# Two-layer backbone on one core: stores whose data ScalarE wrote last move from SyncE's DMA queue to ScalarE's own

## The chip, the cores and the metric

One Trainium2 chip, one of its cores. A core has TensorE (PE), VectorE (DVE), ScalarE (ACT), GpSimd (POOL) and SyncE (SP). SP does nothing but issue DMA transfers. ACT and POOL can issue them too. The metric is the device time of one execution, in microseconds.

## The reference

Two layers over 512 latent and 256 context tokens of 1024 channels. Each layer projects the normed tokens once, runs differential attention and a bidirectional gated DeltaNet on the result, merges both, and then runs PEER: every token picks, for each of 8 heads, 16 of 16384 experts. An expert is one row of `u` and one row of `v`.

```python
y = sigmoid(gA) * (da @ w_ba) + sigmoid(gB) * (dn @ w_bb);  x = x + gate1 * (y @ w_o)
# PEER, per block of 128 tokens; ib: 128 expert numbers of a token, gb: their gates
u   = jnp.take(u_tab, ib, axis=0)
act = jax.nn.gelu(jnp.einsum('tnd,td->tn', u, hb), approximate=False)
v   = jnp.take(v_tab, ib, axis=0)
out = jnp.einsum('tn,tnd->td', gb * act, v)
```

## The kernel before, in words

Matmul operands are split into a high and a low part, and each product takes three matmuls (high by high, low by high, high by low). A tile of a table comes by DMA into `wraw`, `uraw` or `vraw`; ACT casts the high part (`whi`, `uhi`, `vh`, line 189, here "L189"), and POOL or DVE subtracts to get the low part (`wlo`, `ulo`, `vl`, L167). PE multiplies at L160 and transposes at L164. ACT moves most results from PSUM to SBUF (L185, L189, L475, L1349).

The stretches of the span, with the times of the profiled execution: the mixer of layer 0 (0 to 1550 us), its PEER with routing first (1620 to 2260) and the main loop behind it (to 3450), then the mixer of layer 1 (3460 to 4620, with the merge from about 4430 on), and its PEER (scores from 4620, routing 4860 to 5260, main loop to 6080).

What the kernel writes to DRAM on the way:

- In the mixer, `inproj` writes each projected strip (`ev`) to `raw` or to the merge gates `Ga`. DeltaNet's `prep` writes normed keys, values and queries (`kvn`, `kq`). `da_head` writes one head's attention output (its tile is called `g` in the trace) to `AT`. The merge reads `AT` back into `ya`, ACT casts it to `mWh`, and PE multiplies. `norm_turn` writes the rows of the tokens that are gathered to `hrow`.
- In the routing stretch, `spread` builds a dense map of gates for 128 tokens from one-hot tiles: DVE makes `oh`, PE multiplies, ACT scales the result into `stg`, and each finished `stg` (4 MB) goes to `G` in DRAM, 14 times in all. Beside it run two streams: `own_u` gathers the expert rows of the tokens that are not done densely (POOL issues the gather `gb`, DVE multiplies and sums), and `peer_h` computes the first 80 of 128 blocks of `gelu(u . h)` for the dense tokens and keeps each in DRAM (`He`) until the main loop. These are called the blocks done ahead.
- In the main loop, `own_v` gathers rows of `v`, four tokens at a time, PE sums them, ACT copies the sums (`gev`, L1349), and they go to `own`.

Every transfer but the gathers is issued by SP through `load`, loads and stores in one queue of instructions. An engine executes its instructions in order, so a store on SP that waits for its tile holds what stands behind it.

No order is written by hand. The program goes through a list scheduler, which arranges the instructions of each engine by its own estimate of their times. So a change of the engine of a transfer can rearrange all engines. Tiles are numbered buffers: a tile with `bufs=2` is free again when the readers of its last use are done, and a store is a reader.

Of the kernel before, what the change touches and what calls it, by code (L numbers as in the profile page):

```python
# [108 lines left out]
class Ker:  # L109
# [45 lines left out]

    def load(self, dst, src, eng=None):
        (eng or self.nc.sync).dma_start(dst, src)

    def mm(self, out, lhsT, rhs, start=True, stop=True, **k):
        self.PE.matmul(out, lhsT, rhs, start=start, stop=stop, skip_group_check=True, **k)  # L160
# [200 lines left out]
    def norm_turn(self, pool, y, A, shift, hi, lo, toff, hi_on="v", lo_on="v", rows=None):  # L361
        for c0 in (0, 4):
            pt = self.psum("tp")
            hf = self.t(pool, [128, 4, 128], "nhf", bufs=2)
            for c in range(4):
                self.tr(pt[:, c * 128:(c + 1) * 128], y[:, (c0 + c) * 128:(c0 + c + 1) * 128])
            for c in range(4):
                self.act(hf[:, c], pt[:, c * 128:(c + 1) * 128], AF.Identity, scale=A[:, c0 + c:c0 + c + 1],
                         bias=shift[:, c0 + c:c0 + c + 1])
            ts = slice(toff, toff + 128)  # L370
            self.split(hi[:, c0:c0 + 4, ts], lo[:, c0:c0 + 4, ts], hf, hi_on, lo_on)
            if rows is not None:
                if c0 == 0:
                    hb = self.t(pool, [128, D], "nsq", bufs=1)
                pt = self.psum("tp")
                for c in range(4):
                    self.tr(pt[:, c * 128:(c + 1) * 128], hf[:, c])
                self.S.copy(hb[:, c0 * 128:c0 * 128 + 512], pt)
        if rows is not None:
            self.load(rows, hb)  # L380

    def inproj(self, pool, l, tile_i, hT, T, dst, kind=None):


        ps = self.parts("ip", T)
        self.proj(ps, self.wload(self.I["w_in"][l, tile_i], NCH), hT, step=256)
        u = self.t(pool, [128, 768], "ev", bufs=2)[:, :T]
        if kind == "silu":
            th = self.t(pool, [128, 768], "ev", bufs=2)[:, :T]
        for p, o, n in ps:  # L390
            x = slice(o, o + n)
            if kind == "tanh":
                self.act(u[:, x], p, AF.Tanh, scale=0.5)
            elif kind == "silu":
                self.act(th[:, x], p, AF.Tanh, scale=0.5)
                self.act(u[:, x], p, AF.Copy, scale=0.5)
            else:
                self.act(u[:, x], p, AF.Copy, scale=kind or 1.0)
        if kind == "silu":
            self.stt(u, th, 1.0, u, ALU.add, ALU.mult)  # L400
        self.load(dst[:, :T], u)


    @stream("a")
    def da_head(self, pool, l, h, raw, full, AT, lamc, subc):
        li = 0.8 - 0.6 * math.exp(-0.3 * l)
        TQ_ = 768 if full else 512
# [86 lines left out]
            self.tr(pt[:, i * 128:(i + 1) * 128], o2[:, i * 128:(i + 1) * 128])  # L494
        of = self.t(pool, [128, 768], "g2", bufs=2)
        self.act(of[:, :TQ_], pt[:, :TQ_], AF.Copy, scale=subc)
        self.load(AT[:, h, :], of[:, :TQ_])

    def lam_col(self, keep, pool, l):
        li = 0.8 - 0.6 * math.exp(-0.3 * l)  # L500
# [95 lines left out]
    @stream("p")  # L596
    def dn_prep(self, pool, l, h, wi, raw, cw, full, QKd, Knd, Vnd):

        T = 512 if (wi == 0 and not full) else 768
        nt = T // 128  # L600
        th = self.dn_conv(pool, l, h, raw, wi, cw, T)
        off = [i * 128 + (4 if i >= 4 else 0) for i in range(nt)]
        pt = self.psum("sc")
        for i in range(nt):
            self.tr(pt[:, i * 128:(i + 1) * 128], th[:, off[i]:off[i] + 128])
        p3 = pt[:, :T].rearrange("p (a b) -> p a b", b=128)
        dst = self.t(pool, [128, 6, 128], "kvn", bufs=2)[:, :nt]
        if wi == 2:
            self.act(dst, p3, AF.Copy, scale=0.5)
            self.load(Vnd[h], dst)  # L610
            return
        s2 = self.t(pool, [128, 6, 128], "kvn", bufs=2)[:, :nt]
        ss = self.sm(nt)
        for i in range(nt):
            self.act(s2[:, i], p3[:, i], AF.Square, accum=ss[:, i:i + 1])
        self.ts(ss, ss, 0.25, EPS, ALU.mult, ALU.add)
        r = self.sm(nt)
        self.rsqrt(r, ss, nt)
        self.ts(r, r, 0.5 * (128 ** -0.5 if wi == 0 else 1.0), None, ALU.mult)
        for i in range(nt):  # L620
            self.act(dst[:, i], p3[:, i], AF.Copy, scale=r[:, i:i + 1])
        if wi == 1:
            self.load(Knd[h], dst)
        pb = self.psum("at")
        for i in range(nt):
            self.tr(pb[:, i * 128:(i + 1) * 128], dst[:, i, :])
        kT = self.t(pool, [128, 6, 128], "kq", bufs=1)[:, :nt]
        self.S.copy(kT, pb[:, :T].rearrange("p (a b) -> p a b", b=128))
        self.load(QKd[wi][h][:, :nt], kT)

    def dn_solve(self, pool, U):

# [243 lines left out]
    def mixer(self, l, full, xin, xm, h2, near, hT, S, N):  # L876
# [97 lines left out]
        for h in range(2):  # L974
            u = self.t(ep, [128, 768], "ev", bufs=2)
            for p, o, n in first[h][1]:
                self.S.copy(u[:, o:o + n], p)
            self.load(raw[TDK][h], u)
        with P("dv", N) as pool:
            vec = self.dn_vectors(mp, pool, l, hT)  # L980
        bp = dn.enter_context(P("dnb", S))
# [274 lines left out]
    def spread(self, pool, ixs, gate, i, Gd, tick):  # L1256

        V, pair = self.V, self.pair
        n128 = lambda tag: self.t(pool, [128, 128], tag, bufs=1)

        pt = self.psum("tp")
        for x in range(2):
            self.tr(pt[:, x * 128:(x + 1) * 128], ixs[x])
        self.tr(pt[:, 256:384], gate)
        dup = self.t(pool, [128, 4, 128, 2], "rdup", F16, bufs=2)
        self.S.copy(dup[:, 0:2], pair(pt[:, 0:256].rearrange("p (a b) -> p a b", b=128)))
        g14 = n128("rg14")
        self.act(g14, pt[:, 256:384], AF.Copy, scale=GSCALE)
        g16 = self.t(pool, [128, 128], "rg16", F16, bufs=1)
        self.S.copy(g16, g14)  # L1270
        V.tensor_copy(dup[:, 2], pair(g16))
        self.tt(g14, g14, g16, ALU.subtract)
        V.tensor_copy(dup[:, 3], pair(g14))
        every = lambda k, t: dup[:, k, t:t + 8].unsqueeze(2).broadcast_to([128, 8, 64, 2])
        io = self.iota.rearrange("p (a b) -> p a b", b=2).unsqueeze(1).broadcast_to([128, 8, 64, 2])
        for half in range(2):
            stg = self.t(pool, [128, 128, 64], "stg", bufs=2)
            for t8 in range(8):
                oh = self.t(pool, [128, 3, 8, 128], "oh", F16, bufs=3)
                t = half * 64 + t8 * 8  # L1280
                o4 = oh.rearrange("p k t (a b) -> p k t a b", b=2)
                self.tt(o4[:, 0], io, every(1, t), ALU.is_equal)
                self.tt(o4[:, 1], io, every(0, t), ALU.is_equal)
                self.tt(o4[:, 2], o4[:, 1], every(3, t), ALU.mult)
                self.tt(o4[:, 1], o4[:, 1], every(2, t), ALU.mult)
                n = 8 if t8 % 2 else 4
                for u0 in range(0, 8, n):
                    pg = self.psum("at" if t8 % 2 else "tp")
                    for u in range(n):
                        o = pg[:, u * 128:(u + 1) * 128]  # L1290
                        self.mm(o, oh[:, 0, u0 + u], oh[:, 1, u0 + u], stop=False)
                        self.mm(o, oh[:, 0, u0 + u], oh[:, 2, u0 + u], start=False)
                    v = t8 * 8 + u0
                    self.act(stg[:, :, v:v + n].rearrange("p i t -> p t i"),
                             pg.rearrange("p (t i) -> p t i", i=128), AF.Copy, scale=1.0 / GSCALE)
                tick(1 + t8 % 2)
            self.load(Gd[2 * i + half], stg)


    def fetch(self, src, ix):  # L1300
# [34 lines left out]
    def own_v(self, l, own, out):  # L1335

        for s in range(0, 128, 4):
            bs = []
            for q in range(4):
                bs.append(self.fetch(self.I[f"v{l}"], own["ixT"][:, s + q:s + q + 1]))  # L1340
                if q < 3:
                    yield
            ev = self.t(self.gp, [128, D], "gev", bufs=1)
            for o in (0, 512):
                ps = self.psum("tp")
                for q in range(4):
                    self.mm(ps[32 * q:32 * q + 32, :], own["w"][:, s + q:s + q + 1].broadcast_to([128, 32]),
                            bs[q][:, o:o + 512], tile_position=(0, 32 * q))
                self.S.copy(ev[:, o:o + 512], ps)  # L1349
            self.load(out[s:s + 4, :], ev[0:128:32, :])  # L1350
            yield

    def own_all(self, l, owns, rows, outs):
# [27 lines left out]
    def peer(self, l, hT, h2, hg, rows, groups, ahead, near, S, N):  # L1381
# [12 lines left out]
        with ExitStack() as es:  # L1394
# [4 lines left out]
            with P("rt", N) as pool:  # L1399
# [19 lines left out]
                for b in range(ahead):  # L1419
                    ge = self.peer_h(l, b, hT, TT)  # L1420
                    Hd[b] = self.t(self.dp, [128, TT], f"He{l}_{b}")
                    self.load(Hd[b], ge)
            main = ExitStack()
            gp = main.enter_context(P("pg", N))
            adp = main.enter_context(P("ada", N))
# [214 lines left out]
```

## Time and profile before

| | |
|---|---|
| device time, median of 3 runs | 6079.62 us (6079.35 to 6086.33) |
| the profiled execution: time, span | 6081.79 us, 6080.0 us |
| mean granted TensorE clock | 0.969 |
| PE busy | 5620.5 us, 92% of the span |
| DVE, ACT, POOL busy | 4169.0, 2407.6, 2008.7 us |
| DMA moved | 1253.53 MB, 206 GB/s on the mean |

The median and the profiled execution differ by 2.17 us. PE is idle for 6080.0 - 5620.5 = 459.5 us of the span. Issuing a DMA does not count as busy time.

### The profile page before, as it was taken

Reading aid. Unit: us, or ns where it says so; the run is one execution under the profiler, and the core shown is the slowest. Engines: PE = TensorE matmul, PEld = TensorE weight load, DVE = VectorE, ACT = ScalarE, POOL = GpSimd, SP = SyncE. Lnnn points to the kernel's source line nnn. Section 1 sums busy time; section 2 is a strip of 40 time slices with the busy share of each in tenths; the row PEclk is TensorE's granted clock in tenths of the full one; section 3 lists DMA queues with packets and bytes.
Section 4 is the critical chain, followed back from the end, with each engine's and each line's share of the span. In section 5 each row is a group of like instructions: output and inputs, shape, how many; then the busy total and the mean of one; then the engine's idle time right before and its main releaser. Section 6 shows DMA issues by size and latency. Waiting matters only on the chain. (4 is left out here: it accounts for less than half of the span.)

```text
span 6080.0 us, 98316 instructions
## 1 busy us (share of the span) xinstructions
PE 5620.5 (92%) x36087; PEld 4639.6 (76%) x36087; DVE 4169.0 (69%) x9095; ACT 2407.6 (40%) x4320; POOL 2008.7 (33%) x1833
## 2 busy tenths in 40 slices
PE   8999999998888999999999899999999977599998
PEld 6888888777767787666666588888877977587776
DVE  5889886335789876665644669888745599765445
ACT  4554444323224542222233445444533335333333
POOL 2333333231264313333433433334441153312221
PEclk9999999999999999999999999999999998799999
DMA  5442323542278888998988644322254378977886
GB/s 189 154 141 92 100 94 105 173 154 86 69 256 299 293 307 305 333 346 312 328 302 278 224 144 148 118 96 93 96 168 139 125 262 300 329 241 270 286 277 215
DMA packets 567859, 1253.53 MB, mean 206 GB/s; under 512 B 65936, under 2 KB 228432, under 8 KB 565584
## 3 DMA queue, kind: packets, MB, share of 16 engines
q1 hardware_dynamic: 456784, 844.54, 41.0%
q0 software_dynamic: 110592, 402.70, 18.8%
q8 instruction: 284, 4.65, 0.3%
q14 instruction: 199, 1.63, 0.1%
HBM read 1049.76 MB, written 197.23 MB: 205 GB/s over the span
## 5 line engine op out<-in xcount | busy, mean ns | idle before, releaser
L167 POOL TENSOR_TENSOR wlo<-wraw,whi 128x512 fp32r<-128x512 f32 x418 | 571.9, 1371 | 1390.3 <-ACT whi L189 1257.7
L160 PE MATMUL ip<-hhi,whi 128*128 128x256 f32 x3120 | 736.5, 293 | 28.7 <-ACT ev L185 22.4
L160 PE MATMUL ip<-hlo,whi 128*128 128x256 f32 x3120 | 736.3, 291 | 0.7 <-POOL hlo L167 0.7
L160 PE MATMUL ip<-hhi,wlo 128*128 128x256 f32 x3120 | 729.0, 291 | 4.5 <-POOL wlo L167 4.4
L160 PEld LDWEIGHTS ip<-hhi,whi 128*128 128x128 f32 x3120 | 521.2, 192 | 43.0 <-ACT ev L185 26.2
L167 DVE TENSOR_TENSOR acc<-acc,tp 128x512 f32<-128x512 f32 x366 | 247.8, 684 | 445.5 <-PE tp L160 444.6
L160 PE MATMUL ip<-h2hi,ulo 128*128 128x512 f32 (+1 forms) x1408 | 521.4, 371 | 32.9 <-DVE ulo L167 32.9
L160 PE MATMUL ip<-h2hi,uhi 128*128 128x512 f32 (+1 forms) x1408 | 522.3, 371 | 29.6 <-ACT uhi L189 28.9
L160 PEld LDWEIGHTS ip<-hhi,wlo 128*128 128x128 f32 x3120 | 521.2, 193 | 14.9 <-POOL wlo L167 5.5
L189 ACT CAST uhi<-uraw 128x1024 fp32r<-128x1024 f32 x256 | 269.3, 1052 | 663.9 <-PE ip L160 386.8
L160 PEld LDWEIGHTS ip<-hlo,whi 128*128 128x128 f32 x3120 | 524.1, 192 | 8.9 <-POOL hlo L167 1.0
L160 PE MATMUL ip<-h2lo,uhi 128*128 128x512 f32 (+1 forms) x1408 | 519.4, 369 | 0.0
L1302 POOL DMA_INDIRECT gb<-in_ur_dram,gix x261 | 330.2, 1265 | 517.2 <-DVE gb L181 346.9
L167 DVE TENSOR_TENSOR ulo<-uraw,uhi 128x1024 fp32r<-128x1024 f32 x256 | 312.8, 1222 | 248.4 <-ACT uhi L189 243.0
L189 ACT CAST whi<-wraw 128x512 fp32r<-128x512 f32 x418 | 258.2, 620 | 448.5 <-PE at L160 137.6
L1302 POOL DMA_INDIRECT gc<-in_v_dram,gixT x218 | 229.6, 1053 | 450.0 <-PE tp L160 291.2
L189 ACT CAST Wh<-ge 128x512 fp32r<-128x512 f32 (+1 forms) x256 | 144.3, 565 | 580.4 <-PE tp L160 283.2
L181 DVE SCALAR_TENSOR_TENSOR gb<-gb,ghr 128x1024 f32<-128x1024 f32 x261 | 319.5, 1227 | 79.3 <-DMA gb<-in_ur_dram,gix 79.0
L1302 POOL DMA_INDIRECT gb<-in_v_dram,gixT x166 | 178.8, 1077 | 547.4 <-PE tp L160 453.0
L167 DVE TENSOR_TENSOR vl<-vraw,vh 128x1024 fp32r<-128x1024 f32 x256 | 311.1, 1228 | 61.6 <-ACT vh L189 61.6
L160 PE MATMUL tp<-vh,Wh 128*128 128x512 f32 x744 | 293.7, 399 | 61.2 <-ACT vh L189 46.6
L189 ACT CAST vh<-vraw 128x1024 fp32r<-128x1024 f32 x256 | 263.7, 1046 | 169.4 <-PE sc L160 70.6
(458 smaller groups left out, 14800.2 us busy)
## 6 DMA issues: line engine op xcount, KB each, us to landing
uraw<-in_u_dram SPq DMA_DIRECT2D x256, 512.0 KB
vraw<-in_v_dram SPq DMA_DIRECT2D x256, 512.0 KB
wraw<-in_w_in_dram SPq DMA_DIRECT2D x288, 256.0 KB
G<-stg SPq DMA_DIRECT2D x14, 4096.0 KB
g<-G SPq DMA_DIRECT2D x896, 64.0 KB
adw<-in_w_ada_dram SPq DMA_DIRECT2D x192, 256.0 KB
raw<-ev SPq DMA_DIRECT2D x80, 384.0 KB
He<-ge SPq DMA_DIRECT2D x80, 256.0 KB
```

The lines of the kernel that those rows point to most:

```text
L160: self.PE.matmul(out, lhsT, rhs, start=start, stop=stop, skip_group_check=True, **k)
L167: (eng or self.V).tensor_tensor(out, a, b, op)
L181: eng.scalar_tensor_tensor(out, a, s, b, op0, op1, accum_out=accum)
L189: self.S.copy(hi, src)
L1302: self.G.indirect_dma_start(b, None, src, bass.IndirectOffsetOnAxis(ap=ix, axis=0))
```

## The change

A new method `store` issues on ACT's queue instead of SP's. It takes over the stores whose tile ACT wrote last. The stores whose tile another engine wrote last stay on SP, such as the silu strip in `inproj`.

```diff
+    def store(self, dst, src):
+        self.load(dst, src, self.nc.scalar)
...
-            self.load(rows, hb)
+            self.store(rows, hb)
...
         if kind == "silu":
             self.stt(u, th, 1.0, u, ALU.add, ALU.mult)
-        self.load(dst[:, :T], u)
+            self.load(dst[:, :T], u)
+        else:
+            self.store(dst[:, :T], u)
...
-        self.load(AT[:, h, :], of[:, :TQ_])
+        self.store(AT[:, h, :], of[:, :TQ_])
...
-            self.load(Vnd[h], dst)
+            self.store(Vnd[h], dst)
...
-            self.load(Knd[h], dst)
+            self.store(Knd[h], dst)
...
-        self.load(QKd[wi][h][:, :nt], kT)
+        self.store(QKd[wi][h][:, :nt], kT)
...
-            self.load(raw[TDK][h], u)
+            self.store(raw[TDK][h], u)
...
-            self.load(Gd[2 * i + half], stg)
+            self.store(Gd[2 * i + half], stg)
...
-            self.load(out[s:s + 4, :], ev[0:128:32, :])
+            self.store(out[s:s + 4, :], ev[0:128:32, :])
...
-                    self.load(Hd[b], ge)
+                    self.store(Hd[b], ge)
```

In all 481 transfers change engine: 160 `He`, 96 `own`, 96 to `raw`, 32 to `Ga`, 14 `G`, 16 `AT`, 64 normed keys, values and queries, and 3 `hrow`. SP's list falls from 3267 rows to 2786. No work is added.

SP in the routing stretch of layer 0, where blocks are done ahead. Before, loads of `uraw` and stores of `He` alternate:

```order
L157 DMA He_11_4107_21832<-ge_21830 128x512
L157 DMA uraw_21941<-in_u_dram 128x1024
L157 DMA He_12_4113_21867<-ge_21865 128x512
L157 DMA uraw_21976<-in_u_dram 128x1024
L157 DMA He_13_4119_21902<-ge_21900 128x512
L157 DMA uraw_22011<-in_u_dram 128x1024
```

After, SP's list there holds the loads alone. ACT's list, where before `uhi` and `ge` alternated, now holds at the same place:

```order
L193 CAST uhi_21904<-uraw_21906 128x1024
L189 ACTIVATE ge_21865<-ip_21840 128x512
L157 DMA He_12_4113_21867<-ge_21865 128x512
L193 CAST uhi_21939<-uraw_21941 128x1024
L189 ACTIVATE ge_21900<-sc_21875 128x512
L157 DMA He_13_4119_21902<-ge_21900 128x512
L193 CAST uhi_21974<-uraw_21976 128x1024
```

So each store moved from between two loads on SP to between a result and the next cast on ACT (lines of the changed kernel stand 4 to 6 higher).

PE at the end of layer 1's attention. `at_45500<-vk` is the last product with the values, `at_45542<-cst` the last transposes of attention (their source is the normed output of that head), and `ip`, `sc` are matmuls of the merge. Before, 35 matmul rows of the merge stand between the two; the last of them, the transposes, and what follows:

```order
L160 MATMUL ip_47118<-mWh_9157_46991,whi_47119 128x512
L160 MATMUL ip_47118<-mWl_9158_46992,whi_47119 128x512
L160 MATMUL ip_47118<-mWh_9157_46991,wlo_47120 128x512
L160 MATMUL ip_47118<-mWh_9159_46995,whi_47137 128x512
L160 MATMUL ip_47118<-mWl_9160_46996,whi_47137 128x512
L164 MATMUL at_45542<-cst_66,g_8867_45355 128x128 x4
L160 MATMUL ip_47118<-mWh_9159_46995,wlo_47138 128x512
L160 MATMUL ip_47118<-mWh_9161_46999,whi_47137 128x512
```

After, 7 rows stand between them:

```order
L164 MATMUL at_45500<-vk_45313,aT_45498 128x128 x6
L164 MATMUL ip_47118<-mWh_9159_46995,wlo_47138 128x512
L164 MATMUL ip_47118<-mWh_9161_46999,whi_47137 128x512
L164 MATMUL ip_47118<-mWl_9162_47000,whi_47137 128x512
L164 MATMUL ip_47118<-mWh_9161_46999,wlo_47138 128x512
L164 MATMUL ip_47118<-mWh_9163_47003,whi_47137 128x512
L164 MATMUL ip_47118<-mWl_9164_47004,whi_47137 128x512
L164 MATMUL ip_47118<-mWh_9163_47003,wlo_47138 128x512
L168 MATMUL at_45542<-cst_66,g_8867_45355 128x128 x4
L164 MATMUL at_47022<-mWh_9151_46979,whi_47026 128x512
```

So the transposes moved up against the product on which they depend. Behind them, 28 matmul rows stood before until the first that needs this head's `AT`; now there are 22.

## Rows read from the trace of the kernel before

**Rows 1.** The page: busy time, share and instructions; and the chain that ended last.

```profile
PE 5620.5 (92%) x36087; PEld 4639.6 (76%) x36087; DVE 4169.0 (69%) x9095; ACT 2407.6 (40%) x4320; POOL 2008.7 (33%) x1833
...
PE 17%; DVE 3%; DMA 3%; issue 2%; POOL 1%; ACT 0%; SPq 0%; DVEq 0%; POOLq 0%; ACTq 0%
```

**Rows 2.** Windows of both routing stretches: length, busy PE, PEld, DVE, ACT, POOL, clock, DMA.

```profile
1620.00:2060.00 440.00, 386.31 (x1987) 307.15 (x1987) 406.05 (x1043) 175.17 (x197) 214.59 (x195) 0.94 0.77 267
...
4860.00:5260.00 400.00, 283.95 (x1956) 266.57 (x1954) 353.70 (x674) 172.19 (x188) 168.05 (x148) 0.85 0.82 287
```

**Rows 3.** Timeline at 1705 us: start, duration, engine, operation (x: SP's issues).

```profile
1705.14 1.20 DVE L167 TENSOR_TENSOR ulo<-uraw,uhi 128x1024 fp32r<-128x1024 f32 x1
...
1706.37 0.33 SPq L157 DMA_DIRECT2D uraw<-in_u_dram  x1
...
1706.79 0.38 SPq L157 DMA_DIRECT2D He<-ge  x1
```

**Rows 4.** Tile uraw in the two stretches: what uhi's idle engine waited for.

```profile
  DMA uraw<-in_u_dram: 24.0, 11
```
```profile
  DMA uraw<-in_u_dram: 29.9, 13
```

**Rows 5.** DMA while a `G` store runs (5003 to 5012 us): queue, packets, MB, share.

```profile
q1 hardware_dynamic: 205, 3.07, 79.8%
q0 software_dynamic: 229, 0.85, 26.5%
```

**Rows 6.** The chain of work from 4850 to 5300 us: start, duration, what.

```profile
4882.47 7.68 DMA gb<-in_ur_dram,gix
...
5001.20 15.23 DMA gb<-in_ur_dram,gix
```

**Rows 7.** Tile views, issues on SP: ns min/median/max, first and last start.

```profile
L157 SPq DMA_DIRECT2D He<-ge x160: 319/326/1207, 1632.3 to 5186.7; - x160
```
```profile
L157 SPq DMA_DIRECT2D own<-gev x96: 499/500/612, 2326.5 to 6022.7; - x96
```
```profile
L157 SPq DMA_DIRECT2D raw<-ev x96: 319/320/1117, 70.9 to 4230.9; - x96
```
```profile
L157 SPq DMA_DIRECT2D Ga<-ev x32: 319/326/1334, 934.2 to 4441.3; - x32
```

**Rows 8.** PE's waits over the span: us in total, times, longest.

```profile
PE tp L160 <- ACT vh L189: 46.6, 3, 31.8
...
PE ip L160 <- ACT uhi L189: 28.9, 21, 4.6
PE ip L160 <- ACT ev L185: 22.4, 14, 4.3
...
PE at L164 <- ACT kvn L185: 5.8, 8, 1.6
PE sc L160 <- ACT ge L185: 5.2, 5, 1.5
...
PE tp L160 <- ACT gev L1349: 2.6, 4, 0.8
```

**Rows 9.** Timeline at 1704 us: two matmuls of a block done ahead.

```profile
1704.73 0.39 PE L160 MATMUL sc<-h2hi,uhi 128*128 128x512 f32 x1
...
1704.95 0.39 PE L160 MATMUL sc<-h2lo,uhi 128*128 128x512 f32 x1
```

**Rows 10.** Timeline, end of layer 1's attention (waits in brackets).

```profile
4491.58 1.50 PE L160 MATMUL at<-vk,aT 128*128 128x128 f32 x12
...
4495.76 0.25 ACT L475 COPY g<-at 128x128 f32<-128x128 f32 x1
...
4502.80 0.60 PE L164 MATMUL at<-cst,g 128*128 128x128 f32 x4
```
```profile
4503.44 0.69 ACT L185 ACTIVATE g<-at,subc 128x512 f32<-128x512 f32 x1 [1.26 <-PE at L164]
...
4510.59 0.62 ACT L189 CAST mWh<-ya 128x512 fp32r<-128x512 f32 x1 [1.90 <-DMA ya<-AT]
```

## The prediction, written before the changed kernel ran

> **What bounds the kernel now.** I read the page first. PE is busy 92% of the span, and the chain that ended last names PE before all others [rows 1]. SP and ACT's own queue have 0% of that chain. So the gain from a lighter SP can only lie in the roughly 460 us in which PE is idle.
>
> I then read windows, stretch by stretch, to see where PE is idle. The two routing stretches, 840 us together, hold 53.7 + 116.1 = 170 us of it (440 - 386.3 and 400 - 284.0), and DVE is busy 92% and 88% of them [rows 2]. There DVE and the gathers set the pace, not PE and not SP. The other 290 us lie scattered over mixers and main loops.
>
> Next, the timeline of SP: does a load stand behind a store that waits? In the block shown, DVE's `ulo` ends at 1705.14 + 1.20 = 1706.34 and frees the buffer; SP issues the next `uraw` at 1706.37; `He` goes behind it [rows 3]. The load is 0.03 us late, not microseconds. It waits for its buffer, not for the store. The neighbouring blocks that I looked at in that stretch read the same way. Where `ge` ends early it goes out early, and where it ends late the load's buffer comes free later still.
>
> Last, PE's waits that ACT ends, because ACT takes over the work [rows 8].
>
> **The change part by part.** All terms are against the profiled execution, 6081.79 us, which is 2.17 us above the median.
>
> *SP without 481 stores.* What is saved on the path is the lateness of loads. At 0.03 us for each of the 160 blocks done ahead (as many as `He` stores [rows 7]) it is 5 us at the most, and mostly hidden, since DVE sets the pace. Bounds: 0 and -5. I take -1.
>
> *`G` on a ring of its own.* A `G` store is 4 MB. While one runs, the hardware queue moves 3.07 MB in 205 packets, 15 KB a packet, and the gathers' queue 0.85 MB in 229, 3.7 KB a packet [rows 5]. Both took about equally many turns; the queue with big packets got 3.6 times the bytes. A gather that meets a `G` store takes 15.23 us, one before it 7.68 [rows 6]. So queues share by packets. Before, `uraw` stands in one ring behind `G`; after, it takes its own turns. But its packets are small beside those of `G`, so while `G` runs it gets a small share, and it mostly lands when `G` is done, as now.
>
> The Trainium skill says this too ("DMA: Bandwidth & Descriptors", section "Queues, rings and completion order"): each engine goes round the queues that have work, a packet at a time. The rows agree with it.
>
> What can be had at most is ACT's idle time in front of `uhi` that a `uraw` load ends: 24.0 + 29.9 = 53.9 us in 24 places [rows 4]; few of them follow a `G` store (there are 14), and in a stretch that DVE sets PE gets only part. The other way, three queues instead of two take turns, and a gather on the chain can be 1 us later at each of 14 stores. Bounds: -27 (half of 53.9) and +14. I take -3, near the end at which nothing changes, because the block in rows 3 shows loads that wait for buffers.
>
> *ACT issues 481 transfers.* The time that an issue takes ACT isn't in the trace. The nearest rows are SP's: medians of 0.326, 0.320 and 0.326 us for `He`, `raw` and `Ga`, 0.500 for `own` [rows 7]. 385 x 0.326 + 96 x 0.5 = 174 us of issuing go to an ACT that is busy 40% [rows 1]: its idle time covers it almost everywhere. It costs where PE waits for ACT's next result just behind a store. The rows of PE's waits on ACT for `ev`, `uhi`, `kvn`, `ge` and `gev` are 14 + 21 + 8 + 5 + 4 = 52 waits [rows 8]. If every one had one issue in front of it, 52 x 0.326 = 17 us. Many have none: in the changed order a store stands behind `ge` and ahead of the next `uhi`, but `uhi` is mostly waiting for its data then. Bounds 0 and +17. I take +5.
>
> *Blocks done ahead come later in layer 0.* The order counts show PE with fewer blocks ahead under the one-hot tiles: at the last of the 64 one-hot tiles, 76.1 blocks before, 74.1 after, and two to three fewer at each point that I counted from tile 33 on. Two blocks so leave a stretch where PE is idle anyway and go to where PE is nearly full. A block is 24 matmuls; they follow each other every 0.22 us (1704.73 to 1704.95) [rows 9], so 24 x 0.22 = 5.3 us. Against that DVE loses two `ulo` of 1.20 us [rows 3] in the stretch that it sets: 2 x 5.3 - 2.4 = +8.2. If PE's idle time behind takes them in, 0. I take +4. In layer 1 the count is equal at the end: 0.
>
> *Tail of attention in layer 1.* The last product with the values starts at 4491.58 and takes 1.50 us. From ACT's copy of it (4495.76) over square, sum and scale to PE's transposes (4502.80) the chain takes 7.0 us [rows 10]. Before, 35 matmul rows cover it. After, 7: 7 x 0.22 = 1.5 us. If ACT copies at once, PE stands idle for 7.0 - 1.5 = 5.5 us, and PE's queue is in order, so no matmul goes past the transposes. Behind them, from ACT's output (4503.44) over the store, the load and the cast at 4510.59 [rows 10], the cover shrinks from 28 rows to 22, 6 x 0.22 = 1.3 us. Together +7. Bounds: 0, if the weight loads of the merge use the pause and PE waits less for them, and +12, if the copy waits for ACT's casts as it did before (4495.76 against the product's end at 4493.08, 2.7 us) and the issue stands in the way too. Layer 0's tail has more room: 0.
>
> *The rest.* Attention and projections are interleaved otherwise in both mixers. Nothing in the trace tells the sign; I take 0 with +-15.
>
> Sum: -1 - 3 + 5 + 4 + 7 = +12. 6081.79 + 12 = 6094 against the profiled execution, or 6079.62 + 12 = **6092** against the median.
>
> **The rivals.**
>
> *Loads no longer queue behind stores (faster).* If my reading of SP is from too few blocks, or the rings matter more, half of ACT's 53.9 us in front of `uhi` returns as PE time: -27, which gives 6053. For it speaks that `uhi` waits for a load at 24 places [rows 4] and that DMA is busy 77 and 82% there [rows 2]. Against it: the load is issued within 0.03 us of its buffer [rows 3], and DVE sets the pace.
>
> The Trainium skill has a rule for each side. "Perfetto Trace Analysis", section "DMA Optimizations", suggests one engine for inputs and another for outputs, to let them spread more. "DMA: Bandwidth & Descriptors", section "Issuing engines are not separate DMA queues", says that the transfers share the same 16 engines anyhow and that only the sequencer's time is saved, which is usually small. The row on the load's issue agrees with the second.
>
> *ACT stands in its stores (slower).* In the compiled order 86 of the 96 `own` stores on ACT carry a wait for an earlier transfer of another queue, since SP and ACT take turns on eight semaphores. On SP that wait held loads that mostly were not urgent. On ACT it holds `vh` and `Wh` behind it, which PE needs for every block of the main loop. PE's dearest wait on ACT shows what that costs when it happens: 46.6 us in 3 waits for `vh` [rows 8]. In the trace before, the store comes less than 7 us behind the issue that it would wait for at 26 of the 96 places. It decides if ACT waits longer there than its lead over PE; at 1.5 us for each, 26 x 1.5 = +39: 6119.
>
> *All of it is hidden.* ACT is idle 60% of the time, DVE sets the routing stretches, and the pause in the tail is made up by weight loads that come earlier: 6080.
>
> **How the numbers follow.** 0.2% of 6080 is 12 us, about what a measurement of this kernel can tell from no change: faster is below 6067, slower above 6092. My forecast (a small loss, 6092, by its own bounds 6080 to 6108): 0.45, half of it on either side of 6092. Hidden: 0.20, with 0.05 in the faster part from the interleaving. Faster rival: 0.20. Slower rival: 0.15. So faster 0.25, same 0.22 + 0.15 = 0.37, slower 0.23 + 0.15 = 0.38. The range cuts the outer half of the faster rival and the outer third of the slower one: 6055 to 6130.
>
> **What would show each step.** In the profile after, SP's issues of `uraw` should still come within 0.1 us of the end of `ulo`; ACT's idle time in front of `uhi` that a `uraw` load ends stays above 45 us; DVE stays above 87% busy in both routing stretches. ACT's issues of `He` should take about 0.33 us; PE's waits on ACT for `uhi`, `ge` and `ev` should grow by under 17 us. At the end of layer 1's attention a PE wait of about 5 us in front of the transposes `at<-cst` should stand, ended by DVE. If `vh` or `Wh` on ACT wait behind `own` issues that take microseconds, the slower rival is right. If the gathers under `G` get faster, or the wait for `uraw` vanishes, the faster one. I am wrong above all if the new interleaving in the mixers shifts PE's idle time by more than 15 us.

## The result, and the profile after

The changed kernel takes 6128.17 us (median; 6123.12 to 6135.25, 4 executions) against 6079.49 us for the kernel before, timed beside it (4 executions). The ratio is 1.0079, 95% interval [1.0067, 1.0092]: 48 us slower. Its profiled execution took 6123.12 us, its span is 6121.3 us, and its mean granted clock 0.963.

The page of the changed kernel: busy time, the chain by engine, and the hardware queues (packets, MB, share).

```profile
PE 5632.3 (92%) x36087; PEld 4655.3 (76%) x36087; DVE 4191.6 (68%) x9095; ACT 2405.6 (39%) x4320; POOL 2022.7 (33%) x1833
...
q1 hardware_dynamic: 400576, 670.45, 33.5%
...
q10 hardware_dynamic: 56208, 174.09, 7.3%
...
PE 13%; issue 2%; DMA 2%; DVE 2%; POOL 2%; ACT 0%; SPq 0%; DVEq 0%; POOLq 0%; ACTq 0%
```

The stores did move: a second hardware queue carries 174 MB. PE is busy 12 us more for the same 36087 matmuls [rows 1], and idle 489 us instead of 459.5. So of 41 us between the two profiled spans, 29 are idle time of PE and 12 are longer busy time. This split is that of two single traces: in the runs further down, with the same matmuls, PE's busy time goes from 5612 to 5642 us.

PE's waits over the span of the changed kernel (us, times, longest), and ACT's issues by tile view:

```profile
PE ip L164 <- ACT uhi L193: 41.4, 22, 11.6
...
PE tp L164 <- ACT vh L193: 39.5, 2, 33.1
...
PE sc L164 <- ACT uhi L193: 23.8, 7, 7.8
...
PE at L168 <- ACT kvn L189: 15.7, 11, 2.7
...
PE ip L164 <- ACT ev L189: 13.7, 6, 5.0
...
PE tp L164 <- ACT gev L1355: 2.4, 4, 0.8
```
```profile
L157 ACTq DMA_DIRECT2D He<-ge x160: 326/326/443, 1646.5 to 5232.7; - x160
```
```profile
L157 ACTq DMA_DIRECT2D own<-gev x96: 483/484/1054, 2349.5 to 6063.0; - x96
```

An issue costs ACT what it cost SP [rows 7]. PE waits more for `uhi` and `kvn`, and less for `ev` [rows 8]. These rows alone don't tell whether ACT is late because it issues stores or because its work now comes in another order. The experiments separate the two.

Where the time is lost is read by marks that every trace has: the first cast of `uhi` in a layer's PEER, the issue of its last `G` store, the last cast of `vh` in layer 0. The stretches between them, in us (the rows after the second belong to the experiments below):

```
                               mixer 0  routing 0  loop 0   mixer 1  routing 1  loop 1
before                          1618.8    569.6    1253.4   1178.2    612.1     847.9
after                           1632.6    566.5    1262.7   1192.7    624.7     842.1
old order, stores on ACT        1619.1    571.0    1260.4   1177.4    632.9     847.5
new order, stores on SP         1628.0    570.6    1256.3   1193.5    630.4     843.8
mixers' stores on ACT, free     1627.8    556.0    1249.1   1191.8    622.7     843.6
PEER's stores on ACT, free      1622.4    573.6    1260.3   1179.3    606.4     843.5
new order in mixer 0 alone      1627.2    566.0    1249.4   1178.4    614.1     855.4
new order in mixer 1 alone      1626.3    561.1    1257.1   1194.5    610.9     849.7
new order in both PEERs         1618.9    578.2    1254.6   1180.1    628.7     848.8
tail of mixer 1 alone           1623.4    560.7    1256.0   1183.1    607.0     849.2
best order, stores on SP        1618.3    557.0    1255.6   1173.6    605.3     850.7
best order, all on ACT          1620.6    565.7    1273.1   1179.0    617.6     847.0
best order, He and own on ACT   1619.3    559.9    1269.8   1176.3    611.8     848.6
best order, the rest on ACT     1621.1    561.9    1253.5   1177.5    612.0     850.5
```

The changed kernel loses 14 us in layer 0's mixer, 9 in its main loop, 15 in layer 1's mixer and 13 in layer 1's routing stretch. Single traces differ: with the old order there, mixer 1 takes 1174 to 1180 us in eight traces (the moved tail left out), so its 15 us stand out. Mixer 0 takes 1618 to 1626 with the old order, so its 14 stand out less. Routing 1 takes 605 to 633, so its 13 us say little. A trace is also one execution, and some lie off their run's median: that of the old order with ACT's stores took 6109.91 us against a median of 6083.97, that of the best order with all stores on ACT 6104.70 against 6086.98.

### The profile page after: what moved, and what is told of

It is laid out like the page before. It is cut to its first block, busy times and chain, and to the rows that moved or that the text cites. A ratio compares the mean times of both kernels' runs of the same rounds, so it can differ in the third digit from the quotient of the medians.

```text
span 6121.3 us, 98064 instructions
## 1 busy us (share of the span) xinstructions
PE 5632.3 (92%) x36087; PEld 4655.3 (76%) x36087; DVE 4191.6 (68%) x9095; ACT 2405.6 (39%) x4320; POOL 2022.7 (33%) x1833
## 5 line engine op out<-in xcount | busy, mean ns | idle before, releaser
L164 PEld LDWEIGHTS ip<-h2hi,uhi 128*128 128x128 f32 x1408 | 270.1, 192 | 94.1 <-ACT uhi L193 49.0
```

## The experiments

Two theories. Theory A: the scheduler, given another engine for 481 transfers, wrote another order for all engines, and that order is worse. Theory B: ACT pays for the stores. An order can be held: the kernel is scheduled once with one assignment of stores, and then built with another, with an edge from each instruction to the one that came before it on its engine. The edges only fix the order. In the traces, DVE, ACT (its stores left out) and POOL of the two runs that follow execute the same instructions in the same order as the kernel whose order was held. What holding costs by itself was not timed. Where the held order is nearly the old one and the stores are on SP, the trace has 98317 instructions (the moved tail, below), against 98316 before.

```diff
+            for name in order or ():
+                ins = traced[name]
+                if ins.engine in prev:
+                    tc.add_manual_dep(ins, prev[ins.engine], NoSync)
+                prev[ins.engine] = name
...
-    nc = build(stores_on_act)
+    order = build(stores_of_the_order)
+    nc = build(stores_on_act, order)
```

**Old order, stores on ACT.** 

> All 481 stores on ACT's queue, but every engine keeps the order of the kernel before (PE, DVE and POOL row for row; SP the same without the stores; ACT the same with the stores put in). Theory A, the time comes from the new interleaving that the scheduler made: within 8 us of the kernel before, about 6080. Theory B, ACT pays for the stores (their issue, and waits in front of them): the whole loss stays, about 6125. Half of each: about 6100.

6083.97 us, ratio 1.0008 [0.9999, 1.0017].

**New order, stores on SP.** 

> The mirror image: all stores stay on SP's queue, but every engine keeps the order of the changed kernel. Theory A: the loss is there without ACT issuing anything, about 6120 to 6130. Theory B: about 6080.

6128.28 us, ratio 1.0085 [1.0072, 1.0099]. With no store on ACT the whole loss is there; with all stores on ACT and the old order there is next to none. Theory A holds, theory B falls as the main cause. (Each ratio is against the kernel before, timed beside the run.)

**The scheduler free, a part of the stores.** The sets are `{raw, Ga, kvn, kq, AT}` and `{hrow, He, G, own}`.

> The scheduler is free; only the mixers' stores (raw, Ga, normed keys, values and queries, AT: 208) go to ACT. The changed kernel's trace is late by 14 us at the end of layer 0's mixer and by another 15 at the end of layer 1's. Theory A gives no size, since each set of stores gets an order of its own: anything from 6065 to 6130, and the mixers alone are reordered. If the two mixers behave as in the changed kernel: about 6110.

> The scheduler is free; only PEER's stores (He, G, own and the three hrow: 273) go to ACT. If ACT's waits in front of own and He stores cost what the slower rival said, about 6119. If the routing stretch loses as in the changed kernel (some 6 us in layer 0, 5 in layer 1): about 6090. If nothing but the mixers matters: 6080.

6101.13 us, 1.0040 [1.0025, 1.0056], and 6086.43 us, 1.0013 [1.0001, 1.0024]. Each set gets an order of its own, with losses and gains in other places: in the first, layer 0's routing and main loop took 556.0 + 1249.1 us, 18 less than before. Alone these two don't tell order from queue.

**The new order in one stretch at a time, stores on SP.** The held order is that before, with the instructions of one stretch taken in the changed kernel's order.

```diff
+    new = iter([n for n in build(all_stores) if part[n] == stretch])
+    order = [next(new) if part[n] == stretch else n for n in order]
```

> Stores on SP. The order of the changed kernel in layer 0's mixer alone; all else keeps the order before. Theory C, each stretch costs by itself what it was late in the trace of the new order on SP: +9, 6088. Theory D, the loss of a mixer is taken back behind it, because the routing stretch is set by DVE and the gathers: 6080.

> Stores on SP. The new order in layer 1's mixer alone. Theory C: +15, 6094, with the same tail of attention as in the changed kernel (a window in which PE's clock is granted at 0.91). Theory D: 6080.

> Stores on SP. The new order in both PEER parts (routing and main loop), the order before in both mixers. Theory C: +4 in layer 0 and +12 in layer 1, 6095. If the 14 us that appear in layer 1's routing stretch are no matter of the order: 6083.

Mixer 0: 6092.37 us, 1.0020 [1.0010, 1.0030]. Mixer 1: 6099.25 us, 1.0024 [1.0009, 1.0039]. Both PEERs: 6098.84 us, 1.0028 [1.0018, 1.0038]. The three add up to 0.72%, against 0.85% for the whole order. By the times theory C holds and theory D falls: each of the three costs something by itself. The traces bear C out for mixer 1: 16 us later there, and not made up behind it. For mixer 0 they don't: that trace is 8.4 us late at the end of the mixer, only 0.8 us at the end of layer 0's main loop, and then loses 7.5 us in layer 1's main loop, where the order is the old one. So in this trace the lateness is taken back in layer 0, as D said, and where the 12 us of that run come from stays open. The loss has no single place.

PE's wait for `kvn` in mixer 0 of the run with the new order there alone, and then the same wait over the whole span of the run with the old order and ACT's stores:

```profile
PE at L170 <- ACT kvn L191: 11.3, 7, 3.5
```
```profile
PE at L169 <- ACT kvn L190: 5.6, 6, 2.0
```

PE waits 11.3 us for `kvn` there though ACT issues nothing, and 5.6 us in both mixers together where ACT issues everything in the old order (5.8 before [rows 8]). So also this wait on ACT is one of order.

**The tail of mixer 1.** The changed kernel's trace (PE's timeline, waits in brackets), from the last of the seven matmuls that stand in front of the transposes:

```profile
4532.57 0.39 PE L164 MATMUL ip<-mWh,wlo 128*128 128x512 f32 x1
4536.95 1.09 PE L168 MATMUL at<-cst,g 128*128 128x128 f32 x4 [4.00 <-DVE g L171]
4538.81 0.80 PE L164 MATMUL at<-mWh,whi 128*128 128x512 f32 x1 [0.78 <-ACT g L189]
...
4539.83 0.63 PE L164 MATMUL at<-mWh,wlo 128*128 128x512 f32 x1
4540.26 0.63 PE L164 MATMUL at<-mWh,whi 128*128 128x512 f32 x1
```

The transposes wait 4.00 us for DVE. Behind them a matmul comes every 0.43 us, where [rows 9] show 0.22 us: the granted clock from 4535.2 to 4541.9 is 0.50 (a row below shows it), which is the lower of TensorE's two levels, 1.2 GHz instead of 2.4. The windows from the first matmul of the merge to its last say the same, of the changed kernel and of the one before (length, PE, PEld, DVE, ACT, POOL, clock, DMA):

```profile
4437.00:4577.00 140.00, 127.05 (x544) 98.59 (x544) 65.31 (x105) 54.20 (x99) 60.99 (x43) 0.90 0.42 133
```
```profile
4429.00:4543.00 114.00, 108.44 (x516) 87.15 (x515) 55.27 (x83) 44.25 (x80) 53.88 (x39) 1.00 0.50 160
```

The 0.90 is not the tail's doing alone. The merge of the changed kernel holds three stretches at half clock, and outside them it is at 1.00. Their windows, in the same columns, and PE's timeline at the start of the first two:

```profile
4443.00:4453.20 10.20, 9.15 (x26) 6.84 (x27) 8.01 (x7) 2.61 (x5) 5.81 (x4) 0.50 0.68 245
4511.30:4521.50 10.20, 9.54 (x28) 6.86 (x27) 3.46 (x6) 1.95 (x4) 0.00 (x0) 0.50 0.00 1
4535.20:4541.90 6.70, 4.17 (x11) 3.19 (x12) 1.43 (x6) 0.69 (x1) 0.00 (x0) 0.50 0.12 41
```
```profile
4441.02 0.50 PE L164 MATMUL ip<-mWh,wlo 128*128 128x512 f32 x1 [1.41 <-POOL wlo L171]
...
4444.05 0.79 PE L164 MATMUL ip<-mWl,whi 128*128 128x512 f32 x1 [1.49 <-DVE mWl L171]
```
```profile
4510.40 2.17 PE L164 MATMUL at<-vk,aT 128*128 128x128 f32 x12 [2.92 <-ACT aT L476]
```

Each begins in a pause of PE or within 1 us behind it. Half of PE's busy time in them is about what they cost: an estimate of 2 us for the tail's, and of 9 us for the other two. All three are there in both runs that hold this mixer's order with the stores on SP (the whole new order; mixer 1 alone, with 0.90 in the merge's window). In the eight traces with the old order the merge is at 1.00.

To see what one such pause costs, the transposes alone were moved up in the order before:

```diff
+    order = [n for n in order if n not in turn]      # the four transposes
+    order[at + 1:at + 1] = turn                      # at: the 16th matmul behind the product
```

> Stores on SP, the order before on every engine, and one thing moved: at the end of layer 1's attention PE's four last transposes stand 16 matmul rows behind the last product with the values instead of 35. Theory E, only cover is lost: the transposes wait about 19 x 0.22 = 4 us for DVE, the 19 rows run behind them at the same rate, +4 in the trace. Theory F, the pause also costs TensorE's clock: behind the wait the merge's matmuls follow each other every 0.43 us instead of 0.22 for a while, as they do in the changed kernel, and the window is 8 us longer or more.

6087.48 us, 1.0012 [1.0002, 1.0021]. The trace of that run, at the transposes:

```profile
4494.36 0.39 PE L165 MATMUL sc<-mWh,whi 128*128 128x512 f32 x1
4499.48 1.09 PE L169 MATMUL at<-cst,g 128*128 128x128 f32 x4 [4.73 <-DVE g L172]
...
4500.80 0.63 PE L165 MATMUL sc<-mWh,wlo 128*128 128x512 f32 x1
4501.22 0.63 PE L165 MATMUL sc<-mWh,whi 128*128 128x512 f32 x1
...
4504.20 0.40 PE L165 MATMUL ip<-mWl,whi 128*128 128x512 f32 x1
4504.44 0.40 PE L165 MATMUL ip<-mWh,wlo 128*128 128x512 f32 x1
```

A wait of 4.73 us, then from 4500.80 to 4504.20 eight matmuls at 0.43 us instead of 0.22, which adds 8 x 0.2 = 1.6 us, and the transposes at half rate besides. Theory F holds in kind: from the merge's first matmul to its last it takes 119.5 us there instead of 113.0, so 6.5 and not yet 8. The time of the run, 7 us with an interval from 1 to 13, tells nothing between E and F; the trace does.

**The order that gained.** Layer 0's PEER in the order of the run with the mixers' stores, all else as before, and the stores on SP.

> Stores on SP. Layer 0's PEER in the order that the scheduler made when only the mixers' stores went to ACT; all else keeps the order before. In that run's trace this stretch won back 17 us. If the order did it: about 6062, better than the kernel before. If it only made up for a later start: 6080.

6070.39 us, 0.9986 [0.9975, 0.9997]: some 9 us less than the kernel before, with an interval that ends just below it, and 58 less than the changed kernel. Then the same held order with stores on ACT: all, the 225 that are not `He` or `own`, and those two alone.

> The order of the run before that took layer 0's PEER from the order with the mixers' stores alone, now with all 481 stores on ACT's queue. If the queue is without effect at a given order: the same ratio as with the stores on SP, about 0.9986, 6071. If ACT pays for its stores: 6085 or more.

> The same held order as in the run with the best order; on ACT only the mixers' stores, G and hrow (225), with own and He back on SP. Theory G, at a given order ACT pays only for the stores in which it stands waiting (He and own, 37 us of ACT time in that run's trace, all from layer 0's main loop on): layer 0's main loop falls back from 1273 us to 1256 and the ratio to about 0.9986. Theory H, every issue on ACT costs a little: about half of the loss stays, 0.9996.

> The same held order, only own and He (256) on ACT. Theory G: layer 0's main loop 1265 to 1275 us, ratio about 1.0005, and in the trace ACT stands several microseconds in front of some of these stores. Theory H: about half the loss, 0.9996.

All: 6086.98 us, 1.0005 [0.9996, 1.0014]. The rest: 6077.43 us, 0.9997 [0.9987, 1.0006]. `He` and `own` alone: 6087.47 us, 1.0012 [1.0002, 1.0021]. The times alone don't decide: the rest on ACT reads 0.9997, next to theory H's 0.9996 and with G's 0.9986 just outside its interval, while `He` and `own` alone read 1.0012, with G's 1.0005 inside the interval and H's 0.9996 outside; and the intervals of these two runs still overlap. Layer 0's main loop is plainer: 1255.6 us with the stores on SP, 1253.5 with the rest on ACT, 1269.8 with `He` and `own`, 1273.1 with all. Theory G holds for the loop; whether the rest costs a little elsewhere stays open. ACT's timeline of the run with these two alone:

```profile
2202.27 0.60 ACT L191 ACTIVATE ge<-ip 128x512 f32<-128x512 f32 x1 [4.12 <-PE ip L166]
2213.37 0.33 ACTq L157 DMA_DIRECT2D He<-ge  x1
2213.79 1.04 ACT L195 CAST vh<-vraw 128x1024 fp32r<-128x1024 f32 x1 [10.92 <-DMA g<-G]
...
2838.46 0.59 ACT L1357 COPY gev<-tp 128x512 f32<-128x512 f32 x1 [0.27 <-PE tp L166]
2846.34 0.50 ACTq L157 DMA_DIRECT2D own<-gev  x1
2846.89 1.04 ACT L195 CAST uhi<-uraw 128x1024 fp32r<-128x1024 f32 x1 [7.84 <-DMA g<-G]
```

`ge` is ready at 2202.87 and its store goes out at 2213.37. ACT does nothing in between, though `vh` and `uhi` stand behind. The store carries a wait for an earlier transfer of the other queue, as the slower rival said: SP and ACT use the same eight semaphores in turn for their transfers. The profile books the idle time on a load of `g` from `G`; the semaphore that ACT waits for here was last used by a load of `uraw` that SP issued at 2198.94. In front of 13 of the 256 stores ACT stands more than 1 us, 43 us in all. In the changed kernel it does so in front of 9 `He` and `own` stores, 33 us in all, all of them from 2230 us to the end of that loop. Its dearest one, ACT's timeline and then PE's:

```profile
2223.97 0.60 ACT L189 ACTIVATE ge<-ip 128x512 f32<-128x512 f32 x1 [4.12 <-PE ip L164]
2234.72 0.33 ACTq L157 DMA_DIRECT2D He<-ge  x1
2235.14 1.04 ACT L193 CAST vh<-vraw 128x1024 fp32r<-128x1024 f32 x1 [10.57 <-DMA uraw<-in_u_dram]
```
```profile
2237.18 0.79 PE L164 MATMUL ip<-h2hi,uhi 128*128 128x512 f32 x1 [7.81 <-ACT uhi L193]
```

## Why the prediction was right, and where it was not

The direction and the range hold: slower, and 6128 lies under the upper end of 6130. The forecast of 6092 is 36 us short. The sum held +12; 48 were measured. The forecast's own bounds, 6080 to 6108, are missed. That the range holds is luck: its upper end comes from the slower rival, and that mechanism did not make this time. The direction is in small part earned, by the tail of attention, and for the rest luck, since the term that carried the loss stood in the sum without a sign.

*The step that failed is "The rest".* I gave the new interleaving in both mixers 0 +-15. The order alone is 0.85% (52 us of 6080). Its mixers alone make 0.20% + 0.24% = 0.44%, 27 us, of which the tail of mixer 1 is some 6; its PEERs another 0.28%, 17 us, for which the sum had only the +4 of the blocks done ahead. I had read the order only at the places where I had an argument, and given the rest no sign. The bounds were too narrow.

*Tail of attention, +7.* Right in place and kind: the transposes wait 4.00 us for DVE where I had 5.5. Missing was the clock. Of the 14.5 us that mixer 1 takes longer, PE is busy for 8.8 of them, with the same matmuls. The pause moved by itself costs 6.5 us in the merge's window. So what the tail did is about as large as its term, in part by luck: the pause is shorter than I had it, and the slower matmuls behind it make up for that. The other 8 us or so of mixer 1 lie in the merge too. It starts 976 us into the mixer instead of 988, takes 139 us instead of 113, and has two more stretches at half clock. Neither of these two was run by itself.

*Blocks done ahead, +4.* Not seen: routing 0 takes 566.5 us after and 569.6 before. In the runs with this order of PEER and the stores on SP it took 570.6 and 578.2. So between -3 and +9, not told from 0. Only the last, +8.6, stands behind a mixer 0 that ended when it did before; there it is near the 8.2 that I had worked out for two blocks without cover. It is one trace.

*ACT's issues, +5 (0 to 17).* In the old order 1.0008, which is 5 us with an interval from 0 to 10. The size fits in part by luck, and the reason is only half right: an issue takes 0.326 us as forecast, but what the traces show as paid is the time in front of a few `own` and `He` stores in which ACT stands. In the old order layer 0's main loop takes 7 us more with them on ACT (1260.4), in the changed kernel 6 more than in its order on SP (1262.7 against 1256.3), in the best order 14 and 17.5 more. With these stores on SP that loop goes from 1249 to 1257 us over all traces, so the first two are hardly clear of it, and the last are.

*SP without stores, -1.* Right, as far as loads go. DVE's `ulo` and SP's next load in the changed kernel:

```profile
5186.19 1.22 DVE L171 TENSOR_TENSOR ulo<-uraw,uhi 128x1024 fp32r<-128x1024 f32 x1
...
5187.44 0.33 SPq L157 DMA_DIRECT2D uraw<-in_u_dram  x1
```

5187.41 to 5187.44: 0.03 us, as before [rows 3]. In both routing stretches together all 126 loads of `uraw` are issued within 0.1 us of the last `ulo`. Before, 115 of 129 were; 6 came 1.2 to 3.4 us behind it, and all lateness together is some 16 us, where I had 5 at the most. It brought no gain in time: in the old order the ratio is 1.0008.

*`G` on its own ring, -3.* No gain. ACT's idle time in front of `uhi` that a load of `uraw` ends, in both routing stretches of the changed kernel:

```profile
  DMA uraw<-in_u_dram: 41.4, 9
```
```profile
  DMA uraw<-in_u_dram: 44.9, 8
```

86.3 us, where before it was 53.9 [rows 4]. By the same view it is 58.7 in the old order with the stores on ACT, and 67.6 in the new order with them on SP, so neither the queue nor the order makes all of it. (The stand in front of the `He` store is not in it; that idle time falls on `vh`.) The faster rival is out: ACT did not wait less for loads. At a held order, stores on ACT read 1.0008 in the one order, and 1.0005 against 0.9986 in the other. The Trainium skill ("Perfetto Trace Analysis", section "DMA Optimizations") says that one engine for inputs and another for outputs may allow more spread, above all where there are loops or control flow. These ratios show no such gain here.

*The slower rival* described a mechanism that is there, at 9 stores instead of 26 and with 33 us of ACT's time, of which the main loop paid some 6 (1262.7 against 1256.3). It came to 0.1% in the changed kernel, and to 14 and 17.5 us of the loop in the best order, not to the 39 us that I had worked out. That PE paid for less than ACT stood agrees with an ACT that is mostly ahead of PE in that loop; this was not tested by itself. That the time came near to its 6119 is no sign for it: the new order on SP reads 6128.28 too.

*What I said would show.* PE's waits on ACT for `uhi`, `ge` and `ev` should grow by under 17 us. They grew by 22 (63 to 85, over all their rows); in the old order on ACT they are at 66, in the new order on SP at 72. So some 9 of this is order. The other 13 are nearly all waits for `uhi`; 7.81 of them is the one behind the `He` store above. With `kvn` and `gev` they go from 71 to 103, with 73 in the old order on ACT and 92 in the new order on SP. I also said that I am wrong above all if the new interleaving shifts PE's idle time in the mixers by more than 15 us: it went from 216 to 233 us, by 17. DVE's share in the routing stretches is 92% in layer 0, but 85% in layer 1, under the 87% that I named.

## What to carry to other kernels

Where a scheduler decides the order, an edit has two effects, what it does and the order that the scheduler makes of it; hold the order to see the first one alone, and take the second one for a draw whose spread here was from -0.14% to +0.85%. A store on an engine that computes was cheap here only where no wait stood in front of it: look in the compiled order for waits on other transfers in front of it, and for what stands behind it. A pause of PE can cost more than its length: in the two traces where the transposes waited 4.00 and 4.73 us, the matmuls behind them ran at half the clock for some microseconds.

## What was not expected

One pause of 4.73 us of a PE that was otherwise busy was followed by eight matmuls at half rate, from 4500.80 to 4504.20 us, in a place where the clock was at its full level all through the merge before (1.00). The length of the pause alone does not tell: in the changed kernel a wait of 1.41 us and one of 1.49 stand at the first half-rate stretch, while in the merge before, at 1.00 throughout, PE waited 1.83 us in one place:

```profile
4432.80 0.66 PE L164 MATMUL at<-cst,g 128*128 128x128 f32 x4 [1.83 <-DVE g L167]
```

ACT stood 10 us in front of one store, and the row of the store does not show it: a wait in front of an issue counts neither as busy nor as a row of that issue, which still reads 0.33 us. It only shows as a gap between the end of the instruction ahead and the start of the issue, or as the idle time of the cast behind it.
